# A trunk layer with stick-breaking attention: other products dealt out by each step's own TensorE work, low halves of keys and queries a step later, MLP products rearranged, memory attention written first

## The chip, the cores and the metric

One core of a Trainium2 chip runs the whole kernel. The metric is the device time of one execution in microseconds (us). Before the change it is 2463.18 us, the median of three runs (2460.62 to 2464.71).

## What is computed

One decoder layer on `x` (2048 positions of 1024 values): a 12-head attention and a 4-head attention into a memory of 256 tokens share one input projection and one output projection; a squared-ReLU MLP of width 4096 follows. The heads are 64 wide. Cut to what matters:

```python
proj = x @ w_in_sb[slot]
q, k, v = three slices of proj, split into 12 heads; q_mem = proj[..., 3 * w_sb:]
mix = merge_heads(stick_breaking_attention(q, k, v))
mem_out = memory_attention(q_mem, mem, w_mem_kv[layer])      # softmax over 256 tokens
y = jnp.concatenate([mix, mem_out], axis=-1) @ w_out[layer]
x = layer_norm(DN_ALPHA * x + y, ...)
h = jnp.square(jax.nn.relu(x @ w_up[layer]))
x = layer_norm(DN_ALPHA * x + h @ w_down[layer], ...)
```

Stick-breaking attention weights a key s at query t by `beta[t,s] * prod over s<j<t of (1 - beta[t,j])`, with `beta = sigmoid(q.k / 8)` and s strictly before t. So it needs a running product along the keys, from the query backwards, in the place of a softmax.

## The kernel before

**Number format.** Every large product is made of fp16 halves: an operand is kept as a high part and a low part (the rest after rounding), and three passes (`PASSES`: high by high, high by low, low by high) add up in one accumulation bank. A tile that comes out of a bank and is an operand again is therefore split twice: ACT copies the high part (L161), DVE subtracts it and writes the low part (L162). `split_ps` (L159) does both, one behind the other.

**Stages.** The first stage (to about 204 us) loads and transposes `x` and the memory, and computes memory attention (`mem_attend`, in members of a chunk and two heads each) and the projections of the first pair of heads: per chunk of 512 positions `proj_v`, `proj_k` and `proj_q`, then two members of memory attention. Then comes `attention` (L492) over six pairs of heads (p = 0 to 5), then the out projection, the layer norm and the MLP, in two halves of 1024 positions each.

**Attention by steps.** A step is (p, c, pc, i): pair p, query chunk c, key chunk pc (from c down to 0), and the i-th 128 queries of the chunk. Four steps make a block; with pc = c it is a diagonal block, with narrower steps, otherwise a full one. Iteration n of the loop writes, in this order: what is due (the functions that `later(k, fn)` put off by k iterations, value products and evictions among them); `score` of step n + 1 (six matmuls z, for two heads) and its sigmoid on ACT (`stay`, L447); `scan` of step n on DVE (L455), the running product; `spread` of step n - 1 (ACT writes the high half, L309, POOL the low half, L310, and DMA transposes both; short diagonal steps are transposed on PE into the bank pt); then a share of **other products**: the next pairs' projections, later the out projection. The value products (`gather`, 24 matmuls av of a block together) are due four iterations behind the block's last step (`BEHIND`). Inside `attention` every engine runs its instructions in the order in which they are written; outside it a scheduler sets the order.

**Banks.** In attention z has four banks (two steps of two heads), the other products two (pj), the short transposes one (pt), the value products one (av).

**How other products are dealt.** The units of a stretch cost so and so many columns; `FILL` (L489) gives each step a weight (1.0 for a full step, 0.45, 0.45, 0.85 and 1.1 for the four diagonal ones), and the loop writes products until the share of the weights so far is reached (L526 to L535). A product group of 24 ends in an eviction: `q_chunk` (L256) and `proj_k` (L413) put off `split_ps` by one iteration, so the high and the low part are written one behind the other, ahead of that iteration's sigmoid and scan; `proj_v` (L381) copies on ACT and subtracts on DVE (L401) in one iteration too.

**MLP.** `up` (L778) and `down` (L866) multiply 2 x 2 blocks by a scheme with seven products in place of eight: A11, A12, A22 and the sums S1 to S4 of one operand, against blocks or sums (T1 to T4) of the other. Partial results are added up in the banks ba, bb, bc and in tiles u1, u2, u3 between products. In `down` DVE adds a bank to the accumulator `acc` (L886, L888), POOL a tile (L890).

## Time and profile before

| what | value |
|---|---|
| median of three runs | 2463.18 us (2460.62 to 2464.71) |
| the profiled execution, its own time | 2465.01 us |
| its span in the profile | 2463.3 us |
| mean granted TensorE clock | 0.967 of full speed |
| busy share PE / DVE / ACT / POOL | 92% / 69% / 48% / 42% |

Engines are named as in the profile: PE is the matmul engine TensorE, PEld its weight loads, DVE the vector engine, ACT the scalar engine, POOL is GpSimd, SP issues DMAs. A row of the timeline gives the start, the length, the instruction and, in square brackets, how long the engine was idle before and what ended that. A row of waits says which instruction waited for which. A mean over the whole span hides that the stages have different limits, so the stages are read one by one. Where a granted clock stands, 1.00 is the full 2.4 GHz, and half of it is 1.2 GHz.

### The profile page before, as it was taken

How to read it: one execution, taken by the hardware profiler on the slowest of the kernel's cores; microseconds unless marked ns; L12 is line 12 of the kernel's file. 1: busy time of each engine (PE TensorE's matmuls, PEld its weight loads, DVE VectorE, ACT ScalarE, POOL GpSimd, SP SyncE). 2: the span in 40 equal slices, each digit the busy share in tenths (PEclk: the TensorE clock that was granted, in tenths of full speed). 3: DMA queues.
4: the chain of work that ended last, by engine and by line, in shares of the span. 5: the costliest groups of instructions: out<-in, count | busy, mean ns of one | idle time of the engine just before them, and what ended most of it. 6: DMA issues, size and time to landing. Idle time of an engine off the chain costs nothing.

```text
span 2463.3 us, 34394 instructions
## 1 busy us (share of the span) xinstructions
PE 2265.9 (92%) x12032; PEld 1006.3 (41%) x12032; DVE 1702.5 (69%) x2385; ACT 1182.8 (48%) x2577; POOL 1034.2 (42%) x826
## 2 busy tenths in 40 slices
PE   7987999999989899998699999989999999999996
PEld 5433333333434344334244444434444444444442
DVE  4545777777776776887988888787676444555448
ACT  4455767676675656553544543454334222233321
POOL 0000656555564544664664565355335222211123
PEclk9998999999999999999899999999999999999998
DMA  8234888878887787877743454244466333323311
GB/s 261 41 75 88 147 159 143 160 135 150 154 152 144 157 173 161 164 162 158 249 150 119 161 175 140 95 163 167 141 172 230 103 107 99 102 87 95 107 38 69
DMA packets 606284, 342.02 MB, mean 139 GB/s; under 512 B 487840, under 2 KB 544672, under 8 KB 606112
## 3 DMA queue, kind: packets, MB, share of 16 engines
q1 hardware_dynamic: 606112, 339.84, 55.1%
q8 instruction: 94, 1.54, 0.3%
q14 instruction: 78, 0.64, 0.1%
HBM read 143.65 MB, written 77.59 MB: 90 GB/s over the span
## 4 chain that ended last, share of the span: by engine, by line
PE 45%; DVE 13%; DMA 3%; issue 3%; ACT 2%; POOL 2%; SPq 0%; DVEq 0%; POOLq 0%; ACTq 0%
PE upb L799 8%; PE dnb L875 8%; PE dnc L875 6%; PE dna L875 5%; PE upc L799 4%; PE upa L799 4%; PE op L639 4%; DVE wr L683 2%; PE dn L875 2%; DVE rt L683 2%; DVE acc L603 1%; DVE e L455 1%; PE z L272 1%; PE av L332 1%; DMA wd<-in_w_down_dram 1%
## 5 line engine op out<-in xcount | busy, mean ns | idle before, releaser
L310 POOL TENSOR_TENSOR t<-e,t 128x512 f16<-128x512 f32 (+1 forms) x384 | 431.6, 1148 | 437.5 <-ACT t L309 369.6
L890 POOL TENSOR_TENSOR acc<-acc,v 128x512 f32<-128x512 f32 x168 | 223.2, 1339 | 527.9 <-DVE acc L888 388.4
L799 PEld LDWEIGHTS <-rt 128*128 128x128 f16 x2688 | 268.3, 100 | 390.6 <-issue 86.3
L875 PEld LDWEIGHTS <-hl 128*128 128x128 f16 x2736 | 267.7, 98 | 330.3 <-DVE hl L810 5.5
L455 DVE TENSOR_TENSOR_SCAN e<-z,carry,zero 128x512 f32<-128x512 f32 x288 | 347.8, 1261 | 9.5 <-ACT z L447 8.8
L447 ACT ACTIVATE z<-z 128x512 f32<-128x512 f32 (+1 forms) x480 | 226.3, 514 | 257.6 <-PE z L272 135.9
L799 PE MATMUL upb<-op,rt 128*128 128x512 f16 x1152 | 281.6, 395 | 37.3 <-DVE u L842 28.4
L875 PE MATMUL dnb<-wr,hl 128*128 128x512 f16 x1008 | 243.8, 379 | 0.0
L272 PE MATMUL z<-k,q 64*128 64x512 f16 (+3 forms) x1440 | 195.5, 353 | 50.2 <-DVE e L455 45.5
L309 ACT ACTIVATE t<-e 128x512 f16<-128x512 f32 (+1 forms) x384 | 226.4, 616 | 13.2 <-DMA w<-t 12.2
L799 PE MATMUL upa<-op,rt 128*128 128x512 f16 x768 | 185.4, 388 | 14.9 <-ACT u L832 10.7
L799 PE MATMUL upc<-op,rt 128*128 128x512 f16 x768 | 178.8, 380 | 0.9 <-DVE u L843 0.9
L639 PE MATMUL op<-wo,mx 128*128 128x512 f16 x720 | 172.2, 388 | 1.2 <-DVE acc L646 1.2
L875 PE MATMUL dnc<-wr,hl 128*128 128x512 f16 x672 | 167.9, 379 | 1.2 <-DVE acc L886 1.0
L875 PE MATMUL dna<-wr,hl 128*128 128x512 f16 x672 | 163.8, 380 | 3.3 <-DVE hl L810 3.2
L455 DVE TENSOR_TENSOR_SCAN e<-z,zero 128x128 f32<-128x128 f32 (+1 forms) x192 | 147.0, 805 | 22.7 <-ACT z L447 16.5
L332 PE MATMUL av<-w,v 128*64 128x512 f16 (+3 forms) x1440 | 148.9, 352 | 7.1 <-DMA w<-t 5.9
L252 PE MATMUL pq<-xT,wq 128*128 128x512 f16 x576 | 142.4, 389 | 8.2 <-DVE k L162 5.0
L252 PE MATMUL vp<-xT,wv 128*128 128x512 f16 x576 | 145.6, 395 | 2.3 <-ACT wv L143 2.3
L805 ACT ACTIVATE u<-u 128x512 f32<-128x512 f32 x96 | 60.4, 629 | 164.9 <-DVE u L843 73.1
L252 PE MATMUL kp<-xT,wk 128*128 128x512 f16 x576 | 138.9, 383 | 0.0
L908 ACT ACTIVATE v<-dna 128x512 f32<-128x512 f32 x56 | 32.4, 592 | 214.9 <-POOL acc L890 210.3
(176 smaller groups left out, 3211.1 us busy)
## 6 DMA issues: line engine op xcount, KB each, us to landing
keptdown<-wr SPq DMA_DIRECT2D x106, 256.0 KB, 3.3
wr<-keptdown SPq DMA_DIRECT2D x106, 256.0 KB, 2.9
keptup<-rt SPq DMA_DIRECT2D x48, 512.0 KB, 3.1
rt<-keptup SPq DMA_DIRECT2D x48, 512.0 KB, 3.4
wu<-in_w_up_dram SPq DMA_DIRECT2D x32, 512.0 KB, 4.5
wd<-in_w_down_dram SPq DMA_DIRECT2D x32, 512.0 KB, 4.0
x<-in_x_dram SPq DMA_DIRECT2D x16, 512.0 KB, 10.3
acc<-in_x_dram SPq DMA_DIRECT2D x16, 512.0 KB, 5.4
```

The source lines that it names most:

```text
L252: T.matmul(pp, lhsT=wt[:, a, k, :], rhs=xs(xT, c, b, k), start=n == 0, stop=n == 3 * KT - 1)
L272: T.matmul(banks[h], lhsT=q[rows, a, i * P:(i + 1) * P], rhs=keys(b)[rows], start=n == 0, stop=stop and n == 2)
L309: A.activation(hi, src, AF.Copy)
L310: G.tensor_tensor(lo, src, hi, ALU.subtract)
L332: T.matmul(av[h * HD:(h + 1) * HD, i0 * P:].rearrange("p (t n) -> p t n", n=P), lhsT=vv(h, a), rhs=pT(h, b)[:, i0:, :], start=first and n ...
L447: A.activation(t.z[:, :t.W], t.z[:, :t.W], AF.Sigmoid, scale=-SCORE)
L455: V.tensor_tensor_scan(t.e[:, t.W - 1::-1], t.z[:, t.W - 1::-1], zero[:, 0:1].broadcast_to([P, t.W]), init, ALU.mult, ALU.add)
L639: T.matmul(pp, lhsT=lhs, rhs=W[f"o{k}"][:, kb, n * C:(n + 1) * C], start=m == 0, stop=m == 3 * NKO - 1)
L683: V.scalar_tensor_tensor(lo, src, scale, hi, ALU.mult, ALU.subtract)
L799: T.matmul(bv, lhsT=r[:, a, k, :], rhs=operand(ops, s, b, k), start=start and n == 0, stop=n == 3 * HB - 1, skip_group_check=not start)
L875: mm = T.matmul(bank, lhsT=hl[s][:, g, a, i * P:(i + 1) * P], rhs=wr[r][:, g, b, :], start=start and m == 0, stop=m == 3 * n - 1, skip_gro ...
L890: G.tensor_tensor(sl, sl, u, ALU.add)
```

## The change

- `evict` replaces `split_ps` for keys and queries: the high part is written one iteration behind the products' end, the low part one iteration later still. In `proj_v` the subtraction is put off by one iteration in the same way.
- `FILL` is replaced by `SHARE`, `OWN` and `VALUES`: each iteration is charged with its own TensorE work (1800 to 4300, and 4200 or 6500 more where value products are due), and `deal` hands out the other products so that both together come in even shares. The total stays.
- `up`: u3 takes its first addend from bc right behind S1, S4 stands ahead of A22, and the evictions follow.
- `down`: the products of two row tiles alternate, and u3 is added by POOL in an instruction of its own.
- The first stage: two members of memory attention are written ahead of each chunk's projections, and the projections may also take the bank pt.

```diff
@@ evict(), q_chunk(), proj_k(), proj_v()
+    def evict(hi, lo, pp):
+
+        def high():
+            A.activation(hi, pp, AF.Copy, scale=ISQ)
+            later(1, lambda: V.scalar_tensor_tensor(lo, pp, ISQ, hi, ALU.mult, ALU.subtract))
+
+        later(1, high)
...
-        later(1, lambda: split_ps(q[:, 0, :], q[:, 1, :], pp, ISQ))
+        evict(q[:, 0, :], q[:, 1, :], pp)
...
+            later(1, diff)
+
+        def diff():
             V.tensor_tensor(df[:, 1:], d[:, :C - 1], d[:, 1:], ALU.subtract)
             later(1, split)
...
-        later(1, lambda: split_ps(hi, lo, pp, ISQ))
+        evict(hi, lo, pp)
@@ attention()
-    FILL = (0.45, 0.45, 0.85, 1.1)
+
+    SHARE = (0.62, 0.89, 0.78, 0.96), 1.0
+    OWN = (3100, 4300, 2200, 2500), 1800
+    VALUES = 4200, 6500
     BEHIND = 4
 
     def attention(segments, tail):
@@ -498,17 +512,35 @@
         for blocks, done, units in segments:
             mine = [[Score(p, c, pc, h, i) for h in range(2)] for p, c in blocks for pc in range(c, -1, -1)
                     for i in range(TB)]
-            starts[len(steps)] = units, [FILL[t.i] if t.diag else 1.0 for t, _ in mine], done
+            starts[len(steps)] = units, len(mine), done
             steps += mine
         N = len(steps)
+        share = [SHARE[0][t.i] if t.diag else SHARE[1] for t, _ in steps]
+        own = [OWN[0][t.i] if t.diag else OWN[1] for t, _ in steps]
+        for n, (t, _) in enumerate(steps):
+            if t.i == TB - 1 and n + 1 + BEHIND < N:
+                own[n + 1 + BEHIND] += VALUES[0] if t.diag else VALUES[1]
+
+        def deal(begin, count, total):
+
+
+            mine = range(begin, begin + count)
+            low, high = 0, 10 * (total + sum(own))
+            for _ in range(60):
+                rate = (low + high) / 2
+                parts = [max(0, rate * share[n] - own[n]) for n in mine]
+                low, high = (rate, high) if sum(parts) < total else (low, rate)
+            return [sum(parts[:k + 1]) for k in range(count)]
+
         work, spent, total = None, 0, 0
         for n in range(-1, N + BEHIND + 3):
             clock[0] = n
             if n in starts:
                 if work is not None:
                     run(work)
-                units, weight, done = starts[n]
-                begin, spent, total, full = n, 0, sum(k for k, _ in units), sum(weight) * done
+                units, count, done = starts[n]
+                begin, spent, total = n, 0, sum(k for k, _ in units)
+                plan = deal(n, count, total / done)
                 work = (cost for _, u in units for cost in u())
             for fn in due.pop(n, []):
                 fn()
@@ -524,8 +556,7 @@
                     for sblk in range(TB):
                         later(BEHIND, lambda t=t, sblk=sblk: gather(t.p, t.c, t.pc, sblk))
             if work is not None:
-                so_far = sum(weight[:n + 1 - begin]) if n < N else full
-                while spent < total * min(1.0, so_far / full):
+                while spent < min(total, plan[min(n - begin, len(plan) - 1)]):
                     cost = next(work, None)
@@ up()
         prod(bc, S1, rt1, True)
+        u3 = sbt("et", [P, C], F32, f"u3_{nm}")
+        V.tensor_tensor(u3, bc, u1, ALU.add)
         prod(ba, A12, r21, False)
         h11 = sbt("et", [P, C], F32, f"r_{nm}")
         activate(h11, A11, ba)
         prod(bb, S3, rt3, False)
-        u3 = sbt("et", [P, C], F32, f"u3_{nm}")
-        V.tensor_tensor(u3, bb, u1, ALU.add)
-        V.tensor_tensor(u3, bc, u3, ALU.add)
+        V.tensor_tensor(u3, bb, u3, ALU.add)
+        prod(bc, S4, r22, False)
+        V.tensor_tensor(u2, bc, u2, ALU.add)
         prod(bb, A22, rt4, False)
         V.tensor_tensor(u1, bb, u1, ALU.add)
-        prod(bc, S4, r22, False)
-        V.tensor_tensor(u2, bc, u2, ALU.add)
         activate(u3, A22)
@@ down()
         for i0 in range(0, TB, 2):
-            u1 = {}
-            for i in (i0, i0 + 1):
-                ba = pst("bk", f"dna{half}_{i}")
-                prod(i, ba, A11, B11, True)
+            two = (i0, i0 + 1)
+            ba, bb, bc, u1, u2, u3 = {}, {}, {}, {}, {}, {}
+            for i in two:
+                ba[i] = pst("bk", f"dna{half}_{i}")
+                prod(i, ba[i], A11, B11, True)
                 u1[i] = sbt("tt", [P, C], F32, f"v1_{half}_{i}")
-                A.activation(u1[i], ba, AF.Copy)
-                prod(i, ba, A12, B21, False)
-                add(i, c0, 0, ba, None)
-            for i in (i0, i0 + 1):
-                nm = f"{half}_{i}"
-                bb = pst("bk", f"dnb{nm}")
-                bc = pst("bk", f"dnc{nm}")
-                prod(i, bb, S2, T2, True)
-                u2 = sbt("et", [P, C], F32, f"v2_{nm}")
-                V.tensor_tensor(u2, bb, u1[i], ALU.add)
-                prod(i, bc, S1, T1, True)
-                prod(i, bb, S3, T3, False)
-                u3 = sbt("et", [P, C], F32, f"v3_{nm}")
-                V.tensor_tensor(u3, bb, u1[i], ALU.add)
-                add(i, c1, 1, bc, u3)
-                prod(i, bc, S4, B22, False)
-                add(i, c0, 1, bc, u2)
-                prod(i, bb, A22, T4, False)
-                add(i, c1, 0, bb, u1[i])
+                A.activation(u1[i], ba[i], AF.Copy)
+            for i in two:
+                prod(i, ba[i], A12, B21, False)
+                add(i, c0, 0, ba[i], None)
+            for i in two:
+                bb[i] = pst("bk", f"dnb{half}_{i}")
+                prod(i, bb[i], S2, T2, True)
+                u2[i] = sbt("et", [P, C], F32, f"v2_{half}_{i}")
+                V.tensor_tensor(u2[i], bb[i], u1[i], ALU.add)
+            for i in two:
+                bc[i] = pst("bk", f"dnc{half}_{i}")
+                prod(i, bc[i], S1, T1, True)
+                add(i, c1, 1, bc[i], None)
+            for i in two:
+                prod(i, bb[i], S3, T3, False)
+                u3[i] = sbt("et", [P, C], F32, f"v3_{half}_{i}")
+                V.tensor_tensor(u3[i], bb[i], u1[i], ALU.add)
+                sl = acc[c1 * TB + i][:, C:]
+                G.tensor_tensor(sl, sl, u3[i], ALU.add)
+            for i in two:
+                prod(i, bc[i], S4, B22, False)
+                add(i, c0, 1, bc[i], u2[i])
+            for i in two:
+                prod(i, bb[i], A22, T4, False)
+                add(i, c1, 0, bb[i], u1[i])
@@ the first pair's projections
     members = mem_attend()
+    free_banks[0] = ("pj", "pj", "pt")
     for c in range(NC):
+        for _ in range(2):
+            next(members, None)
         for fn in (proj_v, proj_k, proj_q):
             run(fn(0, c))
-        for _ in range(2):
-            next(members, None)
+    free_banks[0] = ("pj",)
```

**PE, a full block** (pair 1, query chunk 3, key chunk 2; z are the scores of the four steps, kp and pq the next pair's key and query products, av the value products; only the first row of each run is shown). Before: 10 other products, av, z, 8, z, 9, z, 9, z.

```order
L272 MATMUL z1_3_2_0_0_4832<-k1_0_2700,q1_2_3330 128x512
...
L252 MATMUL pq2_1_4703<-xT01_1_288,wq2_3566 128x512
...
L332 MATMUL av1_2_4554<-w1_2_0_0_4630,v1_0_2162 64x512
...
L272 MATMUL z1_3_2_1_0_4893<-k1_0_2700,q1_2_3330 128x512
...
L252 MATMUL kp2_2_4857<-xT12_0_383,wk2_3459 128x512
...
L272 MATMUL z1_3_2_2_0_4928<-k1_0_2700,q1_2_3330 128x512
...
L252 MATMUL kp2_2_4857<-xT02_0_382,wk2_3459 128x512
...
L272 MATMUL z1_3_2_3_0_4973<-k1_0_2700,q1_2_3330 128x512
...
L252 MATMUL pq2_2_4965<-xT02_0_382,wq2_3566 128x512
...
L272 MATMUL z1_3_1_0_0_5007<-k1_0_2700,q1_2_3330 128x512
```

With the change: 9 other products, av, z, none, z, 12, z, 11, z.

```order
L280 MATMUL z1_3_2_0_0_4829<-k1_0_2700,q1_2_3356 128x512
...
L252 MATMUL pq2_1_4703<-xT01_1_288,wq2_3565 128x512
...
L340 MATMUL av1_2_4549<-w1_2_0_0_4617,v1_0_2162 64x512
...
L280 MATMUL z1_3_2_1_0_4888<-k1_0_2700,q1_2_3356 128x512
...
L280 MATMUL z1_3_2_2_0_4916<-k1_0_2700,q1_2_3356 128x512
...
L252 MATMUL kp2_2_4857<-xT02_1_412,wk2_3486 128x512
...
L280 MATMUL z1_3_2_3_0_4957<-k1_0_2700,q1_2_3356 128x512
...
L252 MATMUL kp2_2_4857<-xT02_0_382,wk2_3486 128x512
...
L280 MATMUL z1_3_1_0_0_4999<-k1_0_2700,q1_2_3356 128x512
```

The products left the place behind the value products and went to the two places behind it. In other blocks the places hold up to 12, 3, 12 and 11.

**DVE, the same block** (e are the scans; k2_1 is the low half of the next pair's keys, from the bank kp2_2). Before:

```order
L455 SCALAR_TENSOR_TENSOR e1_3_2_1_0_4938<-z1_3_2_1_0_4893,carry_4782,zero_76 128x512
L455 SCALAR_TENSOR_TENSOR e1_3_2_1_1_4940<-z1_3_2_1_1_4894,carry_4782,zero_76 128x512
L162 SCALAR_TENSOR_TENSOR k2_1_4337<-kp2_2_4857,k2_0_4336 128x512
L455 SCALAR_TENSOR_TENSOR e1_3_2_2_0_4983<-z1_3_2_2_0_4928,carry_4782,zero_76 128x512
L455 SCALAR_TENSOR_TENSOR e1_3_2_2_1_4985<-z1_3_2_2_1_4929,carry_4782,zero_76 128x512
L455 SCALAR_TENSOR_TENSOR e1_3_2_3_0_5017<-z1_3_2_3_0_4973,carry_4782,zero_76 128x512
L455 SCALAR_TENSOR_TENSOR e1_3_2_3_1_5019<-z1_3_2_3_1_4974,carry_4782,zero_76 128x512
L455 SCALAR_TENSOR_TENSOR e1_3_1_0_0_5075<-z1_3_1_0_0_5007,carry_4942,zero_76 128x512
L455 SCALAR_TENSOR_TENSOR e1_3_1_0_1_5077<-z1_3_1_0_1_5008,carry_4942,zero_76 128x512
```

With the change:

```order
L466 SCALAR_TENSOR_TENSOR e1_3_2_1_0_4926<-z1_3_2_1_0_4888,carry_4778,zero_76 128x512
L466 SCALAR_TENSOR_TENSOR e1_3_2_1_1_4928<-z1_3_2_1_1_4889,carry_4778,zero_76 128x512
L466 SCALAR_TENSOR_TENSOR e1_3_2_2_0_4967<-z1_3_2_2_0_4916,carry_4778,zero_76 128x512
L466 SCALAR_TENSOR_TENSOR e1_3_2_2_1_4969<-z1_3_2_2_1_4917,carry_4778,zero_76 128x512
L466 SCALAR_TENSOR_TENSOR e1_3_2_3_0_5009<-z1_3_2_3_0_4957,carry_4778,zero_76 128x512
L466 SCALAR_TENSOR_TENSOR e1_3_2_3_1_5011<-z1_3_2_3_1_4958,carry_4778,zero_76 128x512
L260 SCALAR_TENSOR_TENSOR k2_1_4365<-kp2_2_4857,k2_0_4364 128x512
L466 SCALAR_TENSOR_TENSOR e1_3_1_0_0_5071<-z1_3_1_0_0_4999,carry_4930,zero_76 128x512
L466 SCALAR_TENSOR_TENSOR e1_3_1_0_1_5073<-z1_3_1_0_1_5000,carry_4930,zero_76 128x512
```

The low half stood ahead of the scans of the block's third step, and now stands behind those of the fourth. Its high half on ACT moved behind the same step's other ACT work too.

**PE, the end of the first stage** (zm and avm are the scores and values of memory attention, pqm its queries, vp0, kp0 and pq0 the first pair's projections, z0_0_0_0_0 the first scores of attention; only the first row of each run). Before:

```order
L252 MATMUL pqm1_3_1973<-xT03_1_536,wqm1_1443 128x512
...
L272 MATMUL zm1_2_0_1856<-kvm_83,qm1_2_1828 128x256
...
L332 MATMUL avm1_1_1721<-pm1_1_1620,kvm_83 64x512
...
L272 MATMUL zm1_3_0_2001<-kvm_83,qm1_2_1828 128x256
...
L272 MATMUL z0_0_0_0_0_2133<-k0_0_618,q0_0_648 128x128
```

With the change:

```order
L252 MATMUL vp0_3_2029<-xT03_0_506,wv0_567 128x512
...
L280 MATMUL zm1_2_0_1767<-kvm_83,qm1_2_1739 128x256
...
L252 MATMUL vp0_3_2029<-xT03_0_506,wv0_567 128x512
...
L340 MATMUL avm1_1_1630<-pm1_1_1529,kvm_83 64x512
...
L252 MATMUL kp0_3_2064<-xT03_0_506,wk0_572 128x512
...
L340 MATMUL avm1_1_1630<-pm1_1_1529,kvm_83 64x512
...
L280 MATMUL zm1_3_0_1912<-kvm_83,qm1_2_1739 128x256
...
L252 MATMUL kp0_3_2064<-xT03_0_506,wk0_572 128x512
...
L252 MATMUL pq0_3_2091<-xT03_0_506,wq0_577 128x512
...
L280 MATMUL z0_0_0_0_0_2133<-k0_0_914,q0_0_944 128x128
```

Between the last scores of memory attention and the first scores of attention nothing stood; now 8 products of keys and 24 of queries stand there, and 6 and 16 more around the values avm1_1. The values avm1_2 follow the first scores of attention in both.

## Rows read from the trace of the kernel before

**Rows 1.** Windows; columns: stretch, length, busy (instructions) per engine, TensorE clock, DMA share, GB/s

```profile
101.00:204.00 103.00, 88.06 (x480) 39.06 (x481) 53.48 (x154) 56.17 (x168) 3.56 (x3) 0.89 0.41 77
204.00:237.00 33.00, 22.25 (x107) 8.84 (x106) 17.07 (x44) 14.94 (x44) 0.24 (x1) 0.74 0.39 80
...
352.00:486.00 134.00, 124.69 (x824) 51.30 (x824) 100.69 (x116) 92.99 (x240) 79.67 (x73) 1.00 0.84 150
...
619.00:762.00 143.00, 130.16 (x828) 52.77 (x827) 107.16 (x118) 98.90 (x254) 85.86 (x78) 0.96 0.83 153
...
953.00:1108.00 155.00, 144.91 (x837) 59.50 (x834) 124.72 (x159) 86.33 (x199) 94.16 (x78) 0.97 0.75 159
...
1180.00:1860.00 680.00, 628.12 (x2828) 282.00 (x2827) 555.07 (x742) 305.60 (x530) 335.75 (x226) 0.96 0.47 157
1860.00:2396.00 536.00, 530.84 (x2446) 239.74 (x2445) 268.27 (x403) 159.54 (x272) 137.37 (x106) 0.99 0.33 105
```

**Rows 2.** Waits, attention of pairs 0 to 3 (237 to 762 us); total, times, longest

```profile
DVE q L162 <- ACT q L161: 30.1, 13, 3.4
PE z L272 <- DVE e L455: 29.5, 42, 3.1
DVE k L162 <- ACT k L161: 27.6, 14, 3.0
...
PE pt L319 <- DVE w L162: 8.0, 12, 1.5
```

**Rows 3.** Timeline, 463 to 480 us; columns: start, length, instruction, count, [idle before, releaser]

```profile
463.88 0.82 PE L272 MATMUL z<-k,q 64*128 64x512 f16 x6
...
467.44 1.90 PE L252 MATMUL kp<-xT,wk 128*128 128x512 f16 x8
...
467.72 0.69 DVE L162 SCALAR_TENSOR_TENSOR q<-pq,q 128x512 f16<-128x512 f32 x1 [1.48 <-ACT q L161]
...
469.66 0.39 PE L272 MATMUL z<-k,q 64*128 64x512 f16 x1 [0.32 <-DVE e L455]
...
470.84 0.82 PE L272 MATMUL z<-k,q 64*128 64x512 f16 x5 [0.79 <-DVE e L455]
...
471.59 2.12 PE L252 MATMUL kp<-xT,wk 128*128 128x512 f16 x9
...
476.22 2.78 PE L332 MATMUL av<-w,v 128*64 128x512 f16 x24
...
478.93 0.82 PE L272 MATMUL z<-k,q 64*128 64x512 f16 x6
```

**Rows 4.** Page, part 5: the scan, and POOL's additions of the MLP's second product

```profile
L890 POOL TENSOR_TENSOR acc<-acc,v 128x512 f32<-128x512 f32 x168 | 223.2, 1339 | 527.9 <-DVE acc L888 388.4
...
L455 DVE TENSOR_TENSOR_SCAN e<-z,carry,zero 128x512 f32<-128x512 f32 x288 | 347.8, 1261 | 9.5 <-ACT z L447 8.8
```

**Rows 5.** Timeline of PE, 98 to 226 us: memory attention and the first pair's projections

```profile
101.47 0.61 PE L272 MATMUL zm<-kvm,qm 64*128 64x256 f16 x4 [2.55 <-ACT qm L161]
...
132.61 8.07 PE L252 MATMUL pq<-xT,wq 128*128 128x512 f16 x24 [4.96 <-DVE k L162]
...
171.89 6.81 PE L252 MATMUL pq<-xT,wq 128*128 128x512 f16 x23 [3.21 <-ACT vd L395]
...
206.40 0.47 PE L272 MATMUL z<-k,q 64*128 64x128 f16 x5 [1.79 <-DVE w L367]
...
224.94 1.09 PE L319 MATMUL pt<-idf,e 128*128 128x128 f32 x4 [4.20 <-DVE w L162]
```

**Rows 6.** Timeline, 38 to 47 us: first projection, and the weights of memory queries

```profile
38.98 5.31 PE L252 MATMUL vp<-xT,wv 128*128 128x512 f16 x16 [2.29 <-ACT wv L143]
...
46.49 1.23 DVE L148 SCALAR_TENSOR_TENSOR wqm<-sqm,wqm 128x1024 f16<-128x1024 f32 x1 [2.60 <-ACT wqm L143]
```

**Rows 7.** Waits, first half of the MLP (1172 to 1900 us)

```profile
PE upb L799 <- DVE u L842: 28.4, 7, 5.4
```

**Rows 8.** Waits, second half of the MLP (1900 to 2396 us)

```profile
ACT v L908 <- POOL acc L890: 141.8, 14, 14.3
```


## The prediction

> **What bounds the kernel now.** The busy shares of the table (PE 92%) hide stages, so I read the windows first [rows 1]: in each, what PE lacks to the stretch's length. The last half of the MLP is full (530.84 of 536 us): a new order can win next to nothing there. In the attention of pairs 1 and 3 PE is idle for 7 to 9% (124.69 of 134, 130.16 of 143), yet DVE is not full either (100.69 of 134). Two engines that are both free in part, while each waits for the other, are a matter of order. The first stage is worst: 88.06 of 103 us busy at a granted clock of 0.89, then 22.25 of 33 at 0.74.
>
> The waits of 237 to 762 us say who meets whom [rows 2]: scores z wait 29.5 us for scans to free their bank, short transposes 8.0 us for DVE. DVE in turn waits 30.1 and 27.6 us for ACT to write the high parts of queries and keys. The timeline shows one such chain [rows 3]: DVE stands idle for 1.48 us until it can make the low part of q at 467.72; the scans behind it are late, and z waits 0.32 and 0.79 us at 469.66 and 470.84.
>
> **Part 1, low parts a step later.** Nothing is added; each low part of keys and queries and each subtraction of values moves behind a step's scans. The high part on ACT then has a whole step to come, so DVE's 57.7 us of waits go. Their worth is what they delay on PE: z's 29.5 us. Nobody needs a low part soon, since it belongs to the next pair. What is late next is the bank: pj has two, and each is now held about a step longer. A unit of 24 products takes 24 x 0.22 = 5.3 us (0.22 is the step from 8 products in 1.90 to 9 in 2.12 [rows 3]) and spans some 2.7 steps at 8 to 10 products each; a bank is wanted again one unit after its end and is free after two steps. So in pairs 0 to 3 it costs nothing. In the last stretches, where up to 16 products stand in a step, a unit takes 1.5 steps and its bank could be missed for half a step of 15.05 / 4 = 3.8 us (the block below): 1.9 us for each of 12 units, 22 at most. I take 0, since the product that waits stands between scores already written and scores that wait for the same scan anyway; 22 stays as a bound. The Trainium skill speaks against this edit ("PSUM — Partial Sum Buffer", section "Summary: rules for kernel authors"): "Evacuate promptly — 2 MiB is tight." By that rule the 22 us would be paid and the whole change would come to -42 us; no row here shows such a wait.
>
> **Part 2, dealing by own work.** The products are the same; their order decides when DVE gets scores. The full block from z at 463.88 to z at 478.93 takes 15.05 us [rows 3], 1.11 of them z's waits, so PE needs 13.9. DVE needs 8 x 1.261 = 10.1 us for its scans [rows 4] and some 1.7 for the rest (two low parts of 0.69 [rows 3] and odd pieces): 11.8. Neither forbids 13.9 together. The scores have two steps' banks, so DVE can lag by two steps at most. Now the step with value products lasts 1.9 + 2.8 + 0.8 = 5.5 us (8 products, av, z [rows 3]), the others 2.8 to 4.0. With the change it lasts up to 2.6 + 2.8 + 0.8 = 6.2, the next 0.8 to 1.5, the last two 3.4. The short step puts two steps of scores before DVE at once, which it works off (5.0 us) while PE writes products: z's waits go if nothing else holds DVE, and part 1 sees to that. The short transposes wait for DVE as before, and are what is late next.
>
> For parts 1 and 2 together: z's 29.5 us [rows 2], and the clock of pair 3's stretch, where 0.04 x 130 = 5.2 us are lost at 0.96 [rows 1]; 34.7, of which I take **-34**. Bounds: 0, if the waits only move to the value step (below), and -45, if the transposes' 8.0 and some 2 elsewhere go too. In pairs 4 and 5, with out projection and layer norm beside them, DVE is busy for 124.72 of 155 us and PE idle for 10.1 [rows 1]; I take **-6** (0 to -10).
>
> **Part 3, memory attention first.** It gives PE 22 to 32 products to do while ACT and DVE make the softmax. Before, PE stands with nothing: 2.55 us at 101.47, 4.96 at 132.61, 3.21 at 171.89 [rows 5], 10.7 together, which go; 10.75 idle in 204 to 237 us [rows 1] (1.79 at 206.40, 4.20 at 224.94 among them [rows 5]), of which I take half, 5.0, since the values avm1_2 still come behind the first scores. Behind those waits the clock is lower: 24 products take 8.07 us and 23 take 6.81 [rows 5], where 5.3 and 5.1 would do (4.5 together), and 22.25 us at 0.74 lose 5.8 [rows 1], of which I take 4.8. Sum 25. Against it stands the start: the first product now needs the memory queries' weights, whose low part is made from 46.49 us on, where the first projection begins at 38.98 [rows 6]; some 2 us of transposes fill that gap, so 5.5 are lost. **-20** (-5, if half of the gain doesn't come and the front costs its whole 7.5; -35, if all idle time and low clock of 101 to 237 us go).
>
> **Part 4, the MLP.** The instructions stay the same in number. In the first half A22's products wait seven times, 28.4 us, for the eviction of S3 [rows 7]. The new text puts S4's 12 products (2.6 us) between; but in the engines' orders 25 products stand between S3 and A22 before and after, and 13 DVE instructions between u2 and that eviction in both. DVE is busy for 555.07 of 680 us [rows 1], so its backlog sets the wait. I take **-4** (a seventh of 28.4); bounds +10 and -33 (all of it, with a little of the clock). The second half is full: 0.
>
> **Sum.** -34 - 6 - 20 - 4 = -64 from the profiled execution's 2465.0 us: 2401. That execution lies 1.8 us above the median, so **2399 us** on the median's scale.
>
> **Rivals.**
> - *DVE runs dry behind each value step.* With 6.2 us between two scores, DVE has done its 2.5 us of scans some 3.6 us before the next scores have passed the sigmoid. If nothing makes up for it, a block takes 11.8 + 3.6 = 15.4 us, no less than 15.05 now, and parts 1 and 2 give nothing: 2465 - 20 - 10 = 2435, or 2433 on the median's scale. For it: the longest step gets longer. Against it: the step behind it is short, and 13.9 - 11.8 leaves 2 us per block to catch up.
> - *Banks held longer cost the 22 us above*: 2421. For it stands the page's rule; against it that no product waits for pj's banks in the attention's rows.
> - *The MLP's wait for S3 goes too* (33 us): 2370. For it: S4 stands between in the text; against it: the orders.
> - *Slower: POOL holds up the second MLP product.* Both row tiles of a pair now end together, so POOL's last additions of 1.339 us each [rows 4] bunch there. The next pair's tile v1, one of two buffers, must wait for them before ACT copies the bank and PE adds A12 to it. PE has 26 to 32 products, 6 to 7 us, before that. If POOL ends later than 7 us behind T4's last product, PE waits; at 5 us for each of 14 groups +70, 2465 - 60 + 70 = 2475, or 2473. For it: at that copy ACT now waits 141.8 us for POOL, up to 14.3 at a time [rows 8]. Against it: PE lacks only 5.2 of 536 us meanwhile, and POOL is busy for 137.37 of them [rows 1].
> - *No net change*: the attention's gain comes back as waits for transposed weights, and the front costs what the first stage gains: about 2463.
>
> **How the numbers follow.** Chances: forecast 0.60; DVE dry 0.13; banks 0.08; MLP too 0.08; slower 0.07; no change 0.04. From its terms' bounds the forecast spreads some 20 us either way (2379 to 2419). The range takes that in with 2433 and 2421 and the edge of 2370: 2370 to 2437; slower, no change and some of the ends stay out. A measurement of this kernel tells about 0.2%, 4.9 us, from no change. Faster by more: 0.60 + 0.13 + 0.08 + 0.08 = 0.89, less 0.01 for small gains, 0.88; same 0.05; slower 0.07.
>
> **What would show it.** Right: z's waits for scans from 237 to 762 us under 6 us, DVE's waits for ACT's high parts of k and q under 10 in sum, pairs 1 and 2 in about 125 us each, attention's first scores 10 to 20 us earlier, the MLP's stretches as long as now. Wrong: DVE idle for over 3 us behind each value step, products waiting for the low part of k or q, or PE waiting at A12 for ACT's copy v. The forecast has failed outright if z still waits over 20 us.

## The result, and the profile after

The changed kernel takes 2432.47 us (median of 4 runs, 2429.7 to 2435.25), the kernel before 2463.94 in the same comparison: ratio 0.9877, 95% interval 0.9857 to 0.9898, so 30 us (25 to 35) faster. The forecast was 64 us. Its profiled execution has a span of 2428.3 us.

Where the 35.0 us between the two spans come from is read from marks that both programs have: the first start of a projection on PE, DVE's scans (480 in each) and DVE's 32 evictions u2 of the MLP (numbered in order of time). Times count from the start of the span.

| mark, us | before | changed | gained since the mark above |
|---|---|---|---|
| first projection | 39.0 | 46.7 | -7.7 |
| first scan | 210.4 | 204.4 | 13.7 |
| pair 1's first scan | 356.1 | 343.1 | 7.0 |
| pair 4's first scan | 764.7 | 742.5 | 9.2 |
| last scan | 1103.5 | 1071.6 | 9.7 |
| 1st u2 | 1192.4 | 1161.3 | -0.8 |
| 13th u2 | 1683.9 | 1646.6 | 6.2 |
| 17th u2 | 1861.8 | 1817.3 | 7.2 |
| 19th u2 | 1935.0 | 1900.0 | -9.5 |
| end | 2463.3 | 2428.3 | 0.0 |

The windows of the changed kernel, columns as in [rows 1], answer to the rows there (pairs 1 and 3 are the third and fourth row):

```profile
101.00:198.00 97.00, 96.37 (x563) 43.77 (x562) 56.76 (x154) 55.77 (x165) 3.46 (x3) 0.99 0.43 84
198.00:225.00 27.00, 20.83 (x120) 8.67 (x118) 15.67 (x39) 14.74 (x43) 1.16 (x1) 0.87 0.49 88
343.10:475.60 132.50, 123.57 (x830) 52.20 (x827) 101.45 (x116) 92.43 (x239) 79.77 (x73) 1.00 0.86 152
604.60:742.50 137.90, 124.56 (x813) 52.20 (x811) 105.85 (x117) 96.51 (x252) 86.24 (x77) 0.98 0.85 155
1155.00:1817.00 662.00, 612.48 (x2807) 276.96 (x2805) 548.52 (x739) 310.63 (x531) 323.76 (x226) 0.98 0.47 159
1817.00:1900.00 83.00, 69.59 (x307) 30.61 (x306) 48.11 (x55) 21.75 (x37) 36.14 (x30) 0.92 0.46 163
1900.00:2361.00 461.00, 461.00 (x2138) 209.03 (x2136) 227.60 (x349) 138.11 (x230) 93.78 (x74) 1.00 0.30 93
```

The first stage is full now (96.37 of 97.00 us, clock 0.99, where 88.06 of 103 and 0.89 stood), and the stretch behind the first scores lacks 6.2 us in place of 10.75. Pairs 1 and 3 use PE hardly better than before: it is idle for 8.9 of 132.5 us and 13.3 of 137.9, where it was idle for 9.3 of 134 and 12.8 of 143 [rows 1]. In the first half of the MLP PE's idle time is about what it was (49.5 of 662 us, 51.9 of 680 before), but the clock is 0.98 in place of 0.96. The second half is as full as it was. New is a hole at 1817 to 1900 us: 69.59 of 83.00 at 0.92.

The waits of the changed kernel in pairs 0 to 3 (225 to 740 us), beside [rows 2]:

```profile
DVE e L466 <- ACT z L458: 35.4, 23, 3.7
...
PE z L280 <- DVE e L466: 18.0, 19, 4.3
...
DVE e L466 <- POOL t L318: 17.3, 18, 2.0
...
PE pt L327 <- DVE w L162: 15.8, 14, 1.4
...
DVE k L260 <- ACT k L259: 3.3, 5, 1.0
...
DVE q L260 <- ACT q L259: 1.4, 3, 0.5
```

DVE's waits for high parts of keys and queries are gone (57.7 to 4.7 us), as forecast. What they were to free is not: the scores' waits fall from 29.5 to 18.0 us only, the short transposes' double from 8.0 to 15.8, and DVE now waits 35.4 us for sigmoids and 17.3 for POOL. In the kernel before (237 to 762 us) these two were:

```profile
DVE e L455 <- ACT z L447: 15.4, 19, 2.2
...
DVE e L455 <- POOL t L310: 4.8, 4, 1.4
```

The timeline of a diagonal block of the changed kernel shows how:

```profile
417.01 1.03 PE L252 MATMUL kp<-xT,wk 128*128 128x512 f16 x4
...
417.87 1.89 PE L252 MATMUL pq<-xT,wq 128*128 128x512 f16 x8
...
419.69 2.78 PE L340 MATMUL av<-w,v 128*64 128x512 f16 x24
...
422.40 0.50 PE L280 MATMUL z<-k,q 64*128 64x256 f16 x6
...
423.06 0.66 PE L280 MATMUL z<-k,q 64*128 64x384 f16 x6
...
423.57 1.27 DVE L466 TENSOR_TENSOR_SCAN e<-z,zero 128x256 f32<-128x256 f32 x2 [3.73 <-ACT z L458]
...
423.77 0.39 PE L327 MATMUL pt<-idf,e 128*128 128x128 f32 x2
...
424.00 1.03 PE L252 MATMUL pq<-xT,wq 128*128 128x512 f16 x4
...
427.03 0.63 PE L327 MATMUL pt<-idf,e 128*128 128x128 f32 x4 [1.04 <-DVE w L162]
```

PE writes 12 products and 24 value products between two steps' scores (417.01 to 422.40). Behind 418.3 DVE has nothing left but a low part, and its next scan waits 3.73 us for a sigmoid. The next two steps' scores come at once, with no products between them. Only 4 products and one step's scores then stand between the transposes pt at 423.77 and the next ones, which wait 1.04 us at 427.03 for the ones before to leave their single bank.

### The profile page after: what moved, and what is told of

It is laid out like the page before. It is cut to its first block, busy times and chain, and to the rows that moved or that the text cites. A ratio compares the mean times of both kernels' runs of the same rounds, so it can differ in the third digit from the quotient of the medians.

```text
span 2428.3 us, 34523 instructions
## 1 busy us (share of the span) xinstructions
PE 2237.2 (92%) x12032; PEld 1000.8 (41%) x12032; DVE 1709.7 (70%) x2385; ACT 1185.7 (49%) x2577; POOL 1021.7 (42%) x826
## 4 chain that ended last, share of the span: by engine, by line
PE 58%; DVE 18%; issue 8%; ACT 7%; DMA 5%; POOL 3%; SPq 0%; ACTq 0%; DVEq 0%; POOLq 0%
PE dnb L906 7%; PE upb L830 7%; PE dnc L906 5%; PE dna L906 5%; PE upc L830 5%; PE upa L830 4%; PE pq L252 4%; PE z L280 4%; PE op L670 4%; PE av L340 3%; PE kp L252 3%; PE vp L252 3%; DVE wr L714 2%; DVE e L466 2%; POOL t L318 2%
## 5 line engine op out<-in xcount | busy, mean ns | idle before, releaser
L318 POOL TENSOR_TENSOR t<-e,t 128x512 f16<-128x512 f32 (+1 forms) x384 | 431.6, 1150 | 360.0 <-ACT t L317 293.0
L466 DVE TENSOR_TENSOR_SCAN e<-z,carry,zero 128x512 f32<-128x512 f32 x288 | 350.4, 1265 | 44.5 <-ACT z L458 30.2
L921 POOL TENSOR_TENSOR acc<-acc,v 128x512 f32<-128x512 f32 x112 | 149.9, 1341 | 503.1 <-DVE acc L919 432.4
L830 PE MATMUL upb<-op,rt 128*128 128x512 f16 x1152 | 269.6, 383 | 13.0 <-DVE u L874 6.9
L906 PE MATMUL dnb<-wr,hl 128*128 128x512 f16 x1008 | 236.1, 380 | 0.0
L280 PE MATMUL z<-k,q 64*128 64x512 f16 (+3 forms) x1440 | 186.0, 349 | 32.3 <-DVE e L466 31.7
L830 PE MATMUL upa<-op,rt 128*128 128x512 f16 x768 | 184.8, 389 | 26.3 <-ACT u L863 19.3
L830 PE MATMUL upc<-op,rt 128*128 128x512 f16 x768 | 183.7, 387 | 16.1 <-DVE u L869 16.1
L906 PE MATMUL dna<-wr,hl 128*128 128x512 f16 x672 | 155.0, 380 | 9.7 <-DVE hl L841 9.7
L906 PE MATMUL dnc<-wr,hl 128*128 128x512 f16 x672 | 161.1, 379 | 1.8 <-ACT hl L713 1.1
L252 PE MATMUL vp<-xT,wv 128*128 128x512 f16 x576 | 140.4, 388 | 0.0
L280 PEld LDWEIGHTS <-q 64*128 64x128 f16 x1440 | 55.4, 94 | 148.7 <-issue 104.7
```

Of the source, the lines that this page charges most:

```text
L252: T.matmul(pp, lhsT=wt[:, a, k, :], rhs=xs(xT, c, b, k), start=n == 0, stop=n == 3 * KT - 1)
L280: T.matmul(banks[h], lhsT=q[rows, a, i * P:(i + 1) * P], rhs=keys(b)[rows], start=n == 0, stop=stop and n == 2)
L318: G.tensor_tensor(lo, src, hi, ALU.subtract)
L466: V.tensor_tensor_scan(t.e[:, t.W - 1::-1], t.z[:, t.W - 1::-1], zero[:, 0:1].broadcast_to([P, t.W]), init, ALU.mult, ALU.add)
L830: T.matmul(bv, lhsT=r[:, a, k, :], rhs=operand(ops, s, b, k), start=start and n == 0, stop=n == 3 * HB - 1, skip_group_check=not start)
L906: mm = T.matmul(bank, lhsT=hl[s][:, g, a, i * P:(i + 1) * P], rhs=wr[r][:, g, b, :], start=start and m == 0, stop=m == 3 * n - 1, skip_gro ...
```

## The experiments

**The parts, one by one.** Each kernel is the one before with one part's lines of the diff and nothing else.

Part 1 (low parts a step later):

```diff
...
-        later(1, lambda: split_ps(hi, lo, pp, ISQ))
+        evict(hi, lo, pp)
```

> Kernel before with part 1 alone (low parts of keys, queries and the subtraction of values a step later). Theory A, the dealing gives its gain back by starving DVE behind the value products: part 1 alone is worth more than parts 1 and 2 together were in the changed kernel, where attention from its first scan to pair 4's took 538 us against 554 before. So the stretch is 520 to 532 us here and the time 2425 to 2440 us. Theory B, both parts are needed, as forecast: the stretch is 542 us or more, time 2445 us or more.

Measured: 2448.01 us, ratio 0.9931 (0.9913 to 0.9949); the stretch from the first scan to pair 4's took 545.6 us. Both numbers are those of theory B (542 us or more, 2445 us or more), and theory A falls; yet part 1 alone is worth some 15 us. The waits of PE and DVE in its pairs 0 to 3:

```profile
DVE e L466 <- ACT z L458: 39.2, 27, 3.3
...
DVE e L466 <- POOL t L318: 13.2, 19, 1.0
...
PE z L280 <- DVE e L466: 11.9, 14, 2.3
...
PE pt L327 <- DVE w L162: 6.7, 14, 0.9
```

The scores' waits fall to 11.9 us, but the end of a pair takes part of it back. There FILL leaves the last steps almost without products, and PE reaches the value products (av) before DMA has transposed the weights w:

```profile
480.78 0.60 PE L340 MATMUL av<-w,v 128*64 128x512 f16 x1 [2.12 <-issue]
481.54 5.10 PE L340 MATMUL av<-w,v 128*64 128x512 f16 x23 [0.15 <-DMA w<-t]
```

It waits 2.12 us. The row calls that wait "issue", but transposes of w were still under way: one that began at 477.28 landed 4.16 us later. The 23 matmuls behind the wait take 5.10 us. In the changed kernel the same 23 take 2.75 us at the same place, at a granted clock of 1.00:

```profile
472.83 2.75 PE L340 MATMUL av<-w,v 128*64 128x512 f16 x23 [0.51 <-DMA w<-t]
```

With part 1 alone the granted clock from 479.4 to 483.4 us is 0.51, so behind the wait it is at its lower level.

Part 2 (dealing by own work):

```diff
-    FILL = (0.45, 0.45, 0.85, 1.1)
+    SHARE = (0.62, 0.89, 0.78, 0.96), 1.0
+    OWN = (3100, 4300, 2200, 2500), 1800
+    VALUES = 4200, 6500
...
```

> Kernel before with part 2 alone (dealing by own work). Theory A: the stretch from the first scan to pair 4's first is no shorter than 554 us, rather 555 to 565, the time 2460 to 2475 us. Theory B: 540 to 548 us and 2448 to 2455 us.

Measured: 2479.42 us, ratio 1.0062 (1.0045 to 1.0079), and 563.2 us for the stretch. The stretch is theory A's (555 to 565), the time lies 4 us beyond its range: a loss of some 15 us. The scores' waits grow from 29.5 to 37.5 us:

```profile
PE z L272 <- DVE e L455: 37.5, 41, 5.6
...
DVE k L162 <- ACT k L161: 31.2, 14, 4.8
...
DVE ve L401 <- ACT vd L395: 23.1, 18, 8.9
...
PE pt L319 <- DVE w L162: 12.0, 10, 1.4
```

Parts 1 and 2 together, then with the value products charged to the iteration whose products stand right ahead of them on PE:

```diff
-                own[n + 1 + BEHIND] += VALUES[0] if t.diag else VALUES[1]
+                own[n + BEHIND] += VALUES[0] if t.diag else VALUES[1]
```

> Kernel before with parts 1 and 2 together and nothing else. Part 1 alone took 15 us off, part 2 alone added 16. If the new dealing is a loss even where no scan waits for a low part (theory A), the two together are slower than part 1 alone: 2450 to 2458 us. If part 2 needs part 1 and then gains (theory D, the forecast's view): 2436 to 2446 us, faster than part 1 alone.

> The same with the value products charged one iteration earlier. Theory A: 8 to 20 us faster than parts 1 and 2 as written, 2430 to 2444 us, because scores then come at even distances; if the place of the charge doesn't matter, within 4 us of it. The short transposes' waits fall as well (13 us over pairs 1 to 3 in the changed kernel, 2.5 with the charge earlier); if they alone were the loss, the z waits stay as they are and the gain is 8 to 12 us.

Measured: 2451.68 us together (0.9944, 0.9925 to 0.9963), in theory A's range and not in theory D's: no better than part 1 alone. With the charge earlier it is 2436.89 us (0.9889, 0.9868 to 0.9909). Their waits in pairs 0 to 3, first as written, then charged earlier:

```profile
DVE e L466 <- ACT z L458: 36.9, 24, 3.7
...
PE pt L327 <- DVE w L162: 15.8, 14, 1.6
...
PE z L280 <- DVE e L466: 14.2, 19, 1.6
```

```profile
DVE e L466 <- ACT z L458: 37.8, 33, 4.2
...
PE z L280 <- DVE e L466: 19.3, 16, 5.9
...
PE pt L327 <- DVE w L162: 3.2, 6, 0.7
```

So the place of the charge is worth 15 us, as theory A forecast. But the reason that theory A gave for it is not borne out: DVE waits for sigmoids as long as before (36.9 and 37.8 us), and scores wait more (14.2, then 19.3). What fell is the wait of the short transposes, by 12.6 us: with the charge earlier, products stand again between the narrow steps of a diagonal block. The rival named in the expectation, that these alone were the loss, had the scores' waits unchanged and 8 to 12 us; it comes nearer, but is not the whole either, since half of the gain (7 us) comes in pairs 4 and 5, where the transposes waited only 4.1 us at all. There the scores' waits fall from 13.1 to 9.0 us, and the granted clock is 0.98 in place of 0.97.

Part 3 (memory attention first):

```diff
+        for _ in range(2):
+            next(members, None)
         for fn in (proj_v, proj_k, proj_q):
             run(fn(0, c))
-        for _ in range(2):
-            next(members, None)
```

> Kernel before with part 3 alone (memory attention first). By the changed kernel's trace the first scan comes at 204 us against 210, 7.7 us being lost at the first projection. If that is the part's whole worth, the time is 6 to 14 us below before (some of pair 0's gain belongs to it, since its stall behind the first scores shrinks). If the gain in pair 0 was the other parts' work, only 6.

Measured: 2447.11 us, ratio 0.9938 (0.9914 to 0.9962), 15 us; 20 by the spans. The first scan comes 6.4 us earlier, pair 1's 10.8, so its gain shows in pair 0 too, as the first way had it; that the softmax is then done when scores need the engines would be a reason, but is not shown. The other 9 us of the spans come in later stages that the edit does not touch.

Part 4 (MLP products rearranged):

```diff
...
+        V.tensor_tensor(u3, bb, u3, ALU.add)
+        prod(bc, S4, r22, False)
...
         prod(bb, A22, rt4, False)
...
```

> Kernel before with part 4 alone (products of the MLP in another order). From the first u2 eviction to the end the changed kernel took 1267 us against 1271 before. If this is the part's own, the time here is 0 to 6 us below before; if the gain came from work left over from the attention, 0; a wait of A22 for S3 that only moves to S4 shows as waits of upc for DVE in place of upb.

Measured: 2458.37 us, ratio 0.9984 (0.9964 to 1.0005), but from 2448.22 to 2470.22 in ten runs, where the kernel before has 2460.18 to 2468.27. Its profile is of the shortest execution: from the first u2 to the end it takes 1257.4 us, where the kernel before takes 1270.9 and the changed kernel 1267.0. Something takes these 13.5 us back in other executions.

Where they come from shows in the windows from the first u2 to the 17th, first before, then with part 4 alone:

```profile
1192.40:1861.80 669.40, 620.34 (x2798) 278.93 (x2797) 546.92 (x733) 300.25 (x525) 326.89 (x221) 0.96 0.47 155
```

```profile
1189.10:1847.40 658.30, 607.57 (x2791) 275.21 (x2789) 548.99 (x734) 303.79 (x525) 319.18 (x222) 0.98 0.47 158
```

PE is idle no less (49.1 and 50.7 us), but its busy time is 12.8 us shorter, at the higher clock. So it is in all profiles of this study: the nine with part 4 take 654 to 659 us there at a clock of 0.98 to 0.99, the seven without it 667 to 676 at 0.96 to 0.97.

**The changed kernel without one part, or with one repair.** First without part 2, then without part 4:

```diff
-                while spent < min(total, plan[min(n - begin, len(plan) - 1)]):
+                while spent < total * min(1.0, so_far / full):
...
```

> The changed kernel with the dealing before (parts 1, 3 and 4 alone). Theory A, the new dealing is a loss of its own wherever it stands (it cost 16 us alone): 2415 to 2425 us. Theory D, the new dealing is a loss only where the scans wait for low parts, and a small gain beside part 1, because the last steps of a pair keep products for PE to write while transposed weights are under way: 2434 to 2442 us, and value products at each pair's end wait for the transposes (2 us and a stretch at the lower clock), as in the run with part 1 alone.

```diff
...
+        prod(bb, A22, rt4, False)
...
         prod(bc, S4, r22, False)
...
-        prod(bb, A22, rt4, False)
...
```

> The changed kernel with the MLP's products in the order of before (parts 1 to 3 alone). Parts 1 to 3 gave about 31 us up to the last scan. If part 4 wins 10 to 17 us but the long subtraction takes 12 of them back, this kernel shows no such subtraction and takes 2428 to 2436 us, the same as the changed kernel; the seven waits of A22 for S3's eviction are back (28 us). If part 4 was a gain of its own, 2436 to 2445 us.

Measured: 2422.79 us without part 2, ratio 0.9851 (0.9825 to 0.9877), against 0.9877 with it. The intervals overlap: part 2 gains nothing here that is clear of noise, and a loss is not shown either. In the two profiles the time from the first scan to the last is 867.2 us with part 2 and 869.1 without it. The time is in theory A's range, and theory D falls. Without part 4: 2435.68, ratio 0.9889 (0.9873 to 0.9906), next to the changed kernel's 0.9877 and in the first of the two ranges expected. A22's waits are back, and in the changed kernel they had only moved: first the changed kernel's waits of its MLP's first half (1150 to 1817 us), then those without part 4 (1150 to 1850):

```profile
PE upc L830 <- DVE u L869: 16.1, 7, 2.9
...
PE upb L830 <- DVE u L874: 6.9, 4, 2.2
```

```profile
PE upb L830 <- DVE u L873: 23.4, 7, 5.1
```

In the changed kernel S4 waits 16.1 us where A22 waited 28.4 before [rows 7], and A22 still waits 6.9, while a wait for ACT's copy u rose from 10.7 to 15.1 us. S4's and A22's single waits are shorter (at most 2.9 us, where 5.1 and 5.4 stood), and the granted clock is 0.98 with part 4, 0.96 without. That the shorter waits are why the clock stays up fits, but no run changes the one without the other.

The charge of the value products moved in the whole changed kernel, and an eighth buffer for scan outputs:

> The changed kernel with the value products charged to the iteration whose other products stand right ahead of them on PE (one iteration earlier), so that scores come at even distances. Theory A, DVE runs dry because up to 12 products and the value products stand between two scores: the stretch from the first scan to pair 4's first falls from 538 us to 522 to 532, DVE's waits for ACT's sigmoids in it (35 us) to under 20, and the time to 2410 to 2425 us. Theory C, the scan waits for its output buffers and DVE and PE lose as much wherever the products stand: the stretch stays at 535 to 540 and the time at 2428 to 2436.

```diff
-    BUFS = dict(X=16, g=15, st=3, ws=5, et=7, p2=6, tt=2, pw=4)
+    BUFS = dict(X=16, g=15, st=3, ws=5, et=8, p2=6, tt=2, pw=4)
```

> The changed kernel with eight buffers in place of seven for the scans' outputs and the tiles that part 1 holds a step longer. Theory C: DVE's scans wait 17 us for POOL to have read such a tile (5 before the change), and these waits hold up scores; they fall to under 6 us and the time to 2420 to 2428 us. Theory A: the waits fall too, but DVE then waits for scores in their place, and the time stays within 4 us of 2432.

Measured: 2411.92 us (0.9801, 0.9768 to 0.9835) with the charge earlier. From the first scan to the last it takes 854.5 us, 12.7 less than the changed kernel, and to pair 4's first 532.2. The time is theory A's, but its reason fails again: DVE's waits for sigmoids stay (35.2 us in the window where they were 35.4, not under 20). With the eighth buffer 2418.5 us (0.9831, 0.9814 to 0.9847); DVE's waits for POOL fall from 17.3 us to

```profile
DVE e L466 <- POOL t L318: 6.2, 9, 0.8
```

and the stretch from 538.1 to 534.3. That is 4 us for theory C's buffers; the rest of its gain lies in the MLP, where the 17th to the 19th u2 took 70.6 us in place of 82.7. The edit was not meant for it, but the MLP's tiles u1 to u3 come from the same buffers; whether the eighth one or chance removed the hole there is not shown.

The memory queries' weights loaded first:

```diff
...
+    load_cols(w_in, 3 * SBW, "qm0")
     for k, what in enumerate("vkq"):
         load_cols(w_in, (2 * SBW, SBW, 0)[k], f"{what}0")
```

> The changed kernel with the memory queries' weights loaded ahead of the first pair's. If the 7.7 us by which the first projection came later are the whole price of the front, as the prediction had it, the first projection starts at 39 to 40 us, the first scan at 197 to 199, and the time is 2424 to 2427 us. If the first projections then wait for their own weights instead, the first scan comes at 202 or later and the time is 2430 or more.

Measured: 2428.34 us (0.987, 0.9855 to 0.9884). The first projection starts at 39.0, but the first scan at 202.0: of the 7.7 us only 2.4 arrive. That is the second way's first scan, but not its reason: no first projection waits for its own weights. Most of the lead is lost by 74 us, on the way through the transposes of `x`: behind them 24 products of memory queries begin only 2.7 us earlier than in the changed kernel, and in both kernels the wait ahead of them is for DVE's low part of the transposed `x`. PE then waits for the transposed weights of memory attention, 7.39 us here and 7.17 in the changed kernel. First this kernel's rows, then the changed kernel's:

```profile
39.00 1.04 PE L252 MATMUL pqm<-xT,wqm 128*128 128x512 f16 x4 [0.81 <-ACT wqm L143]
...
74.04 7.03 PE L252 MATMUL pqm<-xT,wqm 128*128 128x512 f16 x24 [1.41 <-DVE xT L162]
...
97.86 0.63 PE L340 MATMUL avm<-pm,kvm 128*64 128x512 f16 x1 [7.39 <-DMA pm<-w]
```

```profile
76.77 6.75 PE L252 MATMUL pqm<-xT,wqm 128*128 128x512 f16 x24 [1.41 <-DVE xT L162]
...
100.29 0.64 PE L340 MATMUL avm<-pm,kvm 128*64 128x512 f16 x1 [7.17 <-DMA pm<-w]
```

**The hole at 1817 to 1900 us.** In the changed kernel one DVE subtraction took 13.82 us there; the same instruction takes 0.68 elsewhere. POOL ran multiplications (L628) and additions (L634) of the last layer norm through all of it, and PE stood for 9.24 us:

```profile
1827.03 1.28 POOL L634 TENSOR_TENSOR acc<-acc,gb 128x512 f32<-128x512 f32 x1
1827.23 13.82 DVE L841 TENSOR_TENSOR hl<-r,hl 128x512 f16<-128x512 f32 x1 [8.69 <-ACT r L839]
...
1828.25 2.51 POOL L628 TENSOR_TENSOR acc<-acc,gb 128x512 f32<-128x512 f32 x2
...
1830.70 9.81 POOL L634 TENSOR_TENSOR acc<-acc,gb 128x512 f32<-128x512 f32 x8
...
1841.11 1.03 PE L906 MATMUL dna<-wr,hl 128*128 128x512 f16 x2 [9.24 <-DVE hl L841]
```

The experiment puts that layer norm's work for the first half's rows on DVE:

```diff
...
-                ln_apply(a, mv[:, j, 0:1], rs[:, j:j + 1], 2 if tb < NT // 2 else 1)
+                ln_apply(a, mv[:, j, 0:1], rs[:, j:j + 1], 0 if tb < NT // 2 else 1, on=V if tb < NT // 2 else G)
```

> The changed kernel with the last layer norm's multiplications and additions of the first half's rows on DVE in place of POOL (the same results, 32 additions and multiplications moved). Theory P, the 13.8 us that one DVE subtraction took at 1827 us in the changed kernel's profile were spent waiting for POOL, which then ran a row of such additions without a gap, and this takes about 12 us from most executions: no DVE instruction takes over 4 us, the stretch from the 17th to the 19th u2 eviction lasts 70 to 75 us in place of 82.7, and the median is 2418 to 2425 us. Rival: the subtraction waited for something else (a buffer, a transfer) that comes at the same time: it is as long as before, or PE waits as long elsewhere, and the median stays at 2428 to 2436.

Measured: 2425.19 us (0.9844, 0.9829 to 0.9858; 2423.3 to 2426.91). No DVE instruction is longer than 3 us, and the stretch takes 67.3 us. From the 13th u2 to the 19th, which takes in the work moved to DVE, it is 241.0 us in place of 253.4. The same subtraction takes its usual time:

```profile
1834.33 0.68 DVE L841 TENSOR_TENSOR hl<-r,hl 128x512 f16<-128x512 f32 x1
```

Such an instruction (13.8 to 15.5 us) stands in four of the six profiles of kernels with part 4 and that layer norm on POOL, and in none of the others. The kernels with this edit and other repairs (the two below) lack it too. So theory P holds, with a smaller gain in the median (7 us, and a median at the upper edge of its 2418 to 2425) than in that stretch of the profile (12); that not every execution is hit would explain it, but is not shown.

**Repairs together**, with the new dealing charged earlier, and with the old dealing:

> The changed kernel with all four repairs: value products charged an iteration earlier, eight buffers for scan outputs, the memory queries' weights first, the first half's layer norm on DVE. If they add up (16, 4, 2 and 12 us by the profiles) the time is 2395 to 2405 us; if the first two are the same wait seen twice, 2402 to 2412.

> The changed kernel with the dealing of before and three of the repairs (eight buffers, memory queries' weights first, first half's layer norm on DVE). The same with the new dealing charged an iteration earlier took 2408 us. Theory A, the repaired dealing is worth something of its own: 2414 to 2424 us here. If the old dealing is as good once the buffers are there: 2404 to 2412.

Measured: 2408.0 us (0.9773, 0.9755 to 0.9791) with the new dealing, the fastest kernel of this study, 55 us below before; 2413.6 (0.9795, 0.9774 to 0.9815) with the old one, which lies between the two ranges expected. The repairs do not add up fully (2395 to 2405 were expected if they did), and the repaired dealing's own worth of some 5 us is not clear of noise.

## Why the prediction was half right

- **Part 1's first half held**: DVE's waits for high parts went, as said. **The step that failed** is the next one in parts 1 and 2, "z's waits go if nothing else holds DVE, and part 1 sees to that", which turned 29.5 us of waits into -34. The scores still wait 18.0 us for scans. One thing that holds DVE in place of the low parts is POOL, which must have read an output tile of the scan before it is written again (4.8 us before in pairs 1 to 3, 15.5 after): with the eighth buffer the scores wait 13.7 us and the stretch is 4 us shorter. DVE's waits for sigmoids grew too (15.4 us before, 35.4 after), but are not shown to hold up PE: with part 1 alone they are 39.2 us, and scores wait 11.9. On PE other waits took the place of the scores'. The new waits are as long as the old: scores, transposes and value products together waited 30.2 us of PE's time in pairs 1 to 3 before, and 29.6 after. So the 9.2 us gained there do not come from fewer waits: PE's idle time went from 30.9 to 30.0 us, its busy time from 377.7 to 369.4. Two to three of them are the clock of pair 3 (0.98, where 0.96 stood); where the rest of the busy time went is not shown. For parts 1 and 2 together -13.8 us were measured (0.9944), not -40.
- **Part 2 was costed with the wrong sign.** Its gain was argued from the step behind the value products; the forecast saw that the longest distance grew from 5.5 to 6.2 us and took it as made up for. Alone it costs 15 us, beside part 1 it gains nothing.
- **"The short transposes wait for DVE as before"** failed by 7.8 us: their 8.0 us became 15.8, since the narrow steps that lost their products are those behind which the transposes stand. With the charge earlier, which gives these steps products again, they wait 3.2.
- **The first rival** (DVE runs dry, 2433 us) gives the measured time to the microsecond, but by luck: it had nothing from parts 1 and 2 in pairs 0 to 3 and 30 us from all else, where the parts alone gave -13.8 (1 and 2), -15 (3) and -4 (4). DVE's waits behind value steps are there (3.73 us), yet moving the charge left their sum unchanged.
- **Part 3** was sized well: -20 forecast, -15 measured (20 by the spans). The later start was seen rightly (7.7 us, where 5.5 to 7.5 were forecast) and overpriced: without it 2.4 us come back.
- **Part 4**: -4 forecast and -4 measured (0.9984, not clear of no change), but by luck: a balance that was not foreseen, of 13.5 us won in an undisturbed execution and some 10 lost where POOL holds DVE. The claim that A22's wait would stay, since DVE's backlog sets it, was nearly right: it moved to S4 (16.1 and 6.9 us, where 28.4 stood). What the forecast did not see is that the same idle time in shorter waits comes with a higher granted clock (0.98 in place of 0.96), and that this is where the gain lies.
- **Banks held longer**: no product of keys, queries or values waits for a bank in all of attention (0.0 us in each group from 204 to 1080 us, pairs 4 and 5 included, and 0.6 for the out projection), so the 22 us were rightly put at nothing. The rule "Evacuate promptly" of the Trainium skill ("PSUM — Partial Sum Buffer", section "Summary: rules for kernel authors") bore no cost that these traces show. **The slower case** did not come where it was placed (A12 does not wait for ACT's copy: PE has no wait at all from 1900 to 2361 us); POOL did hold up the MLP, through DVE.

Of the signs of being right only DVE's waits for high parts came as said (4.7 us). Scores waited 18.0 us, not under 6 (over 20 would have been outright failure), pairs 1 and 2 took 132.5 and 129.0 us, not 125, the first scores came 3.6 us earlier (200.8, where 204.4 stood), not 10 to 20, and the first half of the MLP from its first u2 to the 17th took 656.0 us, not the 669.4 of before. Of the signs of being wrong, DVE's idle time of over 3 us behind value steps is there.

What stays open: what shortened PE's busy time in pairs 1 to 3, what holds the clock higher with part 4, and whether part 2 beside part 1 loses anything at all.

## What to carry to other kernels

A wait that ends last hides the next one: before its whole length is booked as gain, put in its place the next-latest thing that the same instruction needs (here the output buffer and the single transpose bank). Read the granted clock beside the waits: part 4 gained 11 us in the first half of the MLP while PE waited no less. When work is dealt out between dependent steps, count the distance from one step's scores to the next in the order in which the engine runs them, not in the iteration that writes them: the same charge one iteration earlier turned nothing into 15 us. Try the parts of a combined change alone; here one of them, alone, cost what another won.

## What the hardware did that was not expected

DVE's subtraction of two operands in SBUF stood for 13.82 us while POOL ran eleven additions and multiplications one behind the other, and ended 0.54 us behind POOL's last one (1841.05 and 1840.51 us). The Trainium skill ("SBUF — State Buffer", section "Who interferes with whom") says that a DVE instruction with two SBUF inputs contends with a GpSimd instruction that reads SBUF. The same page of the Trainium skill (section "SBUF: two separate sides") says that whichever of the two starts first gets the shared ports for its whole instruction. The trace agrees on who blocks whom (POOL's addition began at 1827.03, DVE's subtraction at 1827.23), but the wait was for the whole row of POOL's instructions, not for one of 1.2 us; in the profile with eight buffers the same instruction came in between two of POOL's and took 0.85 us. And a wait of 2 us at a pair's end cost 2.4 us more through the clock, so products kept back for such a place may be worth more than they are long; no run here tests that by itself.
